# Swapped PSUM bank sets, and four more paired slabs whose combinations are made one by one

## The chip, the cores and the metric

One Trainium2 chip; the kernel runs on one of its cores. The metric is the device time of one execution in microseconds. TensorE (PE in the profile) multiplies, VectorE (DVE) and ScalarE (ACT) convert and add, GpSimd (POOL) and SyncE (SP) mostly issue DMAs.

## The reference

One layer of an encoder over 256 rows of width 2048, in float32: a group of mixers, a cross attention, and a gated MLP, each behind an RMS norm. The change touches the MLP and its last projection:

```python
D_FF = ((8 * D_MODEL // 3 + 255) // 256) * 256      # 5632

def swiglu(h, w_gate_up, w_down):
    gate, up = jnp.split(h @ w_gate_up, 2, axis=-1)
    return (jax.nn.silu(gate) * up) @ w_down
...
    x = x + swiglu(rms_norm(x, norm_g[l, 2]), w_gate_up[l], w_down[l])
return rms_norm(x, final_norm_g)
```

## The kernel before

**Slabs, halves and products.** All weights come in one stream of slabs of 128 x 2048 floats (1 MB), loaded by SP into three `raw` buffers. A slab is used as halves of up to 1024 columns. Each half is turned into two fp32r parts: ACT casts `raw` to `wh` (L135, or L159 in a paired slab), DVE subtracts to get the rest `wl` (L136, L160). A ring of three `wh`/`wl` buffers, and a fourth in an extra pool, lets these conversions run ahead of PE. The activations are split in the same way into a high and a low part. A product, `part` (L431), is three matmuls of 128 x 512: high by `wh` (L433), high by `wl` (L434), low by `wh` (L435).

**Plain and paired slabs.** In `paired_rows` (L452) a letter stands for a slab. N is plain: four row blocks by two halves of the 256 rows, eight products. S is paired: a block of 2 x 2 (two row blocks k, two column blocks) is multiplied by seven products instead of eight, in Strassen's manner. An S needs sums of weights, which `_sums` (L140) makes on DVE in place (L157, four additions of 128 x 512 in down's slabs, and conversions of 1024, 512, 1024 and 1024 columns), and sums of activations, the combination that `combine` (L438) makes of two activation tiles: two additions of 128 x 256, four of 128 x 128, then splits into a tile `z`. With the combination go four temporary tiles (`tmp`, eleven buffers). The second product of an S (`b0`, with `x4`) and the later ones use the combination; the first does not.

**Banks.** A group accumulates into eight PSUM banks: a0, a1, b0, b1 (two column blocks by two halves of the rows) from the pool psG (`gbank`, named pg in the profile), and the four products 1, 5, 6, 7 from psM (`bank`, named pm). When the last S of a group is through, `mixed` adds up 1, 5, 6 and 7; then `first` (`gated` in gate/up, `done` in down) adds a0 and a1; b0 and b1 are added after the group's last slab (`upped`, `done`).

**Gate/up.** After a first group by plain slabs, ten groups j = 1 to 10 follow the plan NNSNSNSN. Each ends in `up`: a product with the gate, a transpose, and a store to HBM. The tiles f[0] to f[43] of the hidden activations come back from there through `fetch` (POOL loads a `tmp`, ACT and DVE split it): 22 during gate/up, 22 during down.

**Down.** Two passes over the 44 tiles f, each for two of the four column blocks, by the two plans of `PASSES`. `rest` are the tiles that no S takes; the plain slabs run through them, first for column block 0, then for 1, and `ready(k)` sees to it that f[k + 2] is there. The last 12 rows of the last column block are held back for `down_end`: a part of x is added by matmuls with `identr` (L1230), then the held products run for row half 0 and row half 1, and the final norm follows each. `before(17)` of the second pass gives the extra buffer back.

**Order.** `Background` keeps generators (`fetch`, `combined`) with due times; `poll` steps one between products where less than OWED = 0.9 us of DVE work is owed by its own count, `drain` runs one to its end. What the code emits is then scheduled: instructions of an engine stand in the order in which a scheduler found them ready, earlier code first, not strictly in the order of the code. `keep_place` pins some.

Of the kernel before, what the change touches and what calls it, by code (L numbers as in the profile page):

```python
# [14 lines left out]
F32R = mybir.dt.float32r  # L15
# [8 lines left out]
P = 128  # L24
R = 256
D = 2048
KT = D // P
DFF = 5632
# [16 lines left out]
GROUP = "NNSNSNSN"  # L45

DOWN = GATE_UP + 80
PASSES = "NNNNNNSNNSNNSNNSNNSNNN", "NNSNSNSNSNSNSNNNNNNNNN"

PAIRED = {a + i for a, plan in [(GATE_UP + 8 * j, GROUP) for j in range(10)] + [(DOWN, PASSES[0]), (DOWN + 22, PASSES[1])]  # L50
          for i, x in enumerate(plan) if x == "S"}
# [153 lines left out]
class Background:  # L205
# [17 lines left out]
    def first(self, g):  # L223

        self.q.sort(key=lambda e: e[0] is not g)
# [29 lines left out]
class Block:  # L255
# [25 lines left out]
    def tt(self, out, a, b, op):  # L281
        self.bg.dve(math.prod(out.shape[1:]))
        self.nc.vector.tensor_tensor(out=out, in0=a, in1=b, op=op)  # L283
# [154 lines left out]
    def combine(self, z, a, b):  # L438

        tt, t, u, v, w = self.tt, *(self.tmp() for _ in range(4))  # L440
        for x, y in ((t, a), (u, b)):
            tt(x, y[:, 0:R].bitcast(F32), y[:, R:512].bitcast(F32), ALU.add)
        yield SOON
        tt(v[:, 0:P], t[:, P:R], u[:, P:R], ALU.subtract)
        tt(w[:, 0:P], t[:, 0:P], t[:, P:R], ALU.subtract)
        tt(v[:, P:R], v[:, 0:P], t[:, 0:P], ALU.subtract)
        tt(w[:, P:R], u[:, 0:P], v[:, P:R], ALU.add)
        yield SOON
        for i, x in enumerate((v, w)):
            self.split2(z[:, i * R:i * R + R], z[:, 512 + i * R:512 + i * R + R], x)  # L450

    def paired_rows(self, w, cols, slots, sums, plan, mixed, first, ready=None, late=0, before=None):  # L452

        st, s, nk = self.st, len(sums), len(slots)
        rest = [k for k in range(nk) if not any(k in ks for ks, _ in sums)]
        steps = [(c, k) for c in range(2) for k in rest]  # L460
        todo, q = iter(sums), {}
        count = {"a0": len(rest) + s, "a1": len(rest) + s, "b0": len(rest) + s, "b1": len(rest)}
        left, total = {}, 0

        def put(name, hi, lo, wh, wl):
            if name not in q:
                q[name] = self.gbank() if name in count else self.bank()
                left[name] = count.get(name, s)
            new = left[name] == count.get(name, s)
            left[name] -= 1  # L470
            self.part(q[name][:, :], hi, lo, wh, wl, new, left[name] == 0)

        form = lambda t, r: (t[:, r * P:(r + 1) * P], t[:, R + r * P:R + (r + 1) * P])
        n = done = 0
        for i, kind in enumerate(plan):
            if before:
                before(i)
            if kind == "S":
                ks, z = next(todo)
                a = [form(slots[ks[0]], 0), form(slots[ks[1]], 0), form(slots[ks[1]], 1)]  # L480
                x1, s2, s3, x4 = ((z[:, i * P:i * P + P], z[:, 512 + i * P:512 + i * P + P]) for i in range(4))
                t = (("5", x1), ("7", s3))
                pairs = iter((("1", a[0]), ("b0", x4), ("a0", a[1]), *(t if st.n // 16 in SUMMED else t[::-1]), ("a1", a[2]), ("6", s2)))
                for parts in st.take_sums(w, ks, cols):
                    for wh, wl in parts:
                        name, (hi, lo) = next(pairs)
                        put(name, hi, lo, wh, wl)
                        self.bg.poll()
                done += 1
                if done == s:  # L490
                    mixed(*(q[i] for i in "1567"))
            else:
                for c, k in steps[n:n + 4]:
                    if ready:
                        ready(k)
                    wh, wl = st.take(w, k, cols[c], 4)
                    for r in range(2):
                        put("ab"[c] + str(r), *form(slots[k], r), wh, wl)
                        self.bg.poll()
                n += 4  # L500
            if first and done == s and n >= len(rest):
                first(q["a0"], q["a1"])
                first = None
        assert n == len(steps) - late and done == s
        return [q["b0"], q["b1"]], rest[len(rest) - late:]
# [527 lines left out]
    def gate_up(self, gp, f, z):  # L1033

        nc = self.nc
        box, g, stored = {}, {}, []
# [6 lines left out]
        def up(j, ps, h=None):  # L1043
            h = h or [gp.tile([P, 512], F32, name="h", tag="h", bufs=2) for _ in range(2)]
            for r in range(2):
                self.stt(h[r], ps[r], box["col"][:, r:r + 1], g[r], ALU.mult, ALU.mult)
                self.store_turned(self.ff, 4 * j, r, g[r], h[r])
            stored.append(self.bg.now)
# [16 lines left out]
        def upped(j, ps):  # L1065

            for r in range(2):
                self.tt(h[r], h[r], ps[r], ALU.add)
            up(j, h, h)
# [34 lines left out]
        def combined():  # L1104
            for ks, z in sums:
# [3 lines left out]
        sums = [((2 * i, 2 * i + 1), z[i]) for i in range(GROUP.count("S"))]  # L1109
# [3 lines left out]
                            before=lambda n: n in (1, 3) and self.bg.drain(self.late if n == 1 else last))  # L1113
# [3 lines left out]
        early = self.bg.add(fetch(0, FT - 22, 3, 2.0, 15))  # L1117
        self.bg.drain(comb)
        for j in range(1, DFF // 512):
            upped(j, self.paired_rows("w_gate_up", [j * 512, DFF + j * 512], self.h3, sums, GROUP, mixed, gated)[0])  # L1120
        self.bg.drain(early)
        self.fetch = self.bg.add(fetch(FT - 22, FT, 6, SOON))

    def down(self, f, sp):

        nc, st = self.nc, self.st
        ss = self.rp.tile([P, 24], F32, name="rc", tag="rc")  # L1130
        self.gap(sp, 192)
        z = [sp.tile([P, 1024], F32R, name=f"y{i}") for i in range(PASSES[1].count("S"))]
        u = sp.tile([P, 512], F32, name="u")
        sums = [((2 * i, 2 * i + 1), x) for i, x in enumerate(z)]
        made, split = [], []

        def combined(n):
            for ks, x in sums[len(made):n]:
                yield from self.combine(x, *(f[k] for k in ks))
                made.append(x)  # L1140
                yield 2.0

        def squares(x, c, r):
            nc.scalar.activation(self.tmp().bitcast(BF16), x, AF.Square, accum_out=ss[:, 4 * r + c:4 * r + c + 1])

        def mixed(c, q1, q5, q6, q7):

            add = lambda a, b: self.tt(a, a, b, ALU.add)
            nc.scalar.copy(u, q1)
            add(self.half(c, 0), u)  # L1150
            add(u, q6)
            v = [(self.tmp(), slice(j, j + R)) for j in range(0, 512, R)]
            for t, j in v:
                self.tt(t, u[:, j], q7[:, j], ALU.add)
            self.tt(u, q5, u, ALU.subtract)
            add(self.half(c + 1, 0), u)
            for t, j in v:
                add(self.half(c, 1)[:, j], t)
                self.tt(t, q5[:, j], t, ALU.subtract)
                add(self.half(c + 1, 1)[:, j], t)  # L1160
            if c:
                for j in range(0, 512, R):
                    parts = [self.tmp().bitcast(F32R) for _ in range(2)]
                    self.split2(*parts, self.half(3, 1)[:, j:j + R])
                    split.append((j, parts))

        def done(c, *ps):

            for r, p in enumerate(ps):
                x = self.half(c, r)  # L1170
                self.tt(x, x, p, ALU.add)
                squares(x, c, r)

        def ready(k):

            while self.have < min(FT, k + 3):
                self.bg.step(next(e for e in self.bg.q if e[0] is self.fetch))

        for i, plan in enumerate(PASSES):
            n = plan.count("S")  # L1180
            g = self.bg.add(combined(n))
            late = (0, LATE)[i]
            plan = plan[:22 - late // 4]

            def before(j):
                if j == plan.index("S"):
                    self.bg.drain(g)
                if late and j == len(plan) - 2:
                    st.extra = None

            ps, rest = self.paired_rows("w_down", [2 * i * 512, (2 * i + 1) * 512], f, sums[:n], plan,
                                        lambda *q: mixed(2 * i, *q), lambda *q: done(2 * i, *q), ready, late, before)
            if i == 0:
                done(1, *ps)
        return ss, ps, rest, split
# [681 lines left out]
```

## Time and profile before

| | us |
|---|---|
| median of 3 runs | 1444.63 |
| runs | 1441.95 to 1446.84 |
| the profiled execution, time | 1443.87 |
| the profiled execution, span of instructions | 1442.1 |

The profile is of one execution; "idle before" and "[... <-X]" say how long the engine had been idle and what ended that. In the profile, down's fetched tiles appear under the names of the buffers that they lie in (act, f, z), combinations of down as y, the temporaries as tmp. The second pass begins at about 1317.4 us, the held end at 1417.2.

### The profile page before, as it was taken

What the parts mean: (1) busy time and instruction counts of PE and PEld (TensorE: products, weight loads), DVE (VectorE), ACT (ScalarE), POOL (GpSimd) and SP (SyncE); (2) the same over time, 40 slices, a digit from 0 to 9 for tenths busy, and PEclk for the clock granted to TensorE, in tenths of its full rate; (3) what the DMA queues carried; (4) which work ended last, traced back from release to release, by engine and by line L of the source; (5) the groups of instructions that cost most, each with busy time, mean ns of one, the idle gap of its engine ahead of it and who ended that gap; (6) DMA issues with size and microseconds to landing.
All of it is one profiled execution on the core that took longest, in us unless ns stands there. A gap on an engine that the chain in (4) does not pass through costs nothing.

```text
span 1442.1 us, 18599 instructions
## 1 busy us (share of the span) xinstructions
PE 1426.6 (99%) x6601; PEld 1183.1 (82%) x6601; DVE 1125.6 (78%) x1681; ACT 807.5 (56%) x1160; POOL 234.8 (16%) x306
## 2 busy tenths in 40 slices
PE   9999999999999999999999999999999999999997
PEld 8888888888888888888888888888888878788886
DVE  6667868777977666676676888889888889978884
ACT  7556655446655555555555555555555556555553
POOL 0000100012312233530421112112211103000000
PEclk9999999999999999999999999999999999999999
DMA  9886564456667788864976998989999877645563
GB/s 357 296 287 242 204 216 152 170 180 220 204 204 222 240 260 266 270 207 153 295 238 206 281 304 272 284 266 279 280 290 294 263 229 266 200 180 193 216 221 130
DMA packets 73039, 343.80 MB, mean 238 GB/s; under 512 B 10958, under 2 KB 12655, under 8 KB 45169
## 3 DMA queue, kind: packets, MB, share of 16 engines
q1 hardware_dynamic: 54848, 288.98, 57.4%
q0 software_dynamic: 17664, 52.97, 15.4%
q8 instruction: 52, 0.85, 0.2%
q10 hardware_dynamic: 432, 0.66, 0.1%
q14 instruction: 43, 0.34, 0.1%
HBM read 322.12 MB, written 20.45 MB: 238 GB/s over the span
## 4 chain that ended last, share of the span: by engine, by line
PE 93%; DVE 3%; DMA 2%; ACT 1%; issue 0%; ACTq 0%; DVEq 0%
PE pg L433 25%; PE pg L435 25%; PE pg L434 25%; PE pg L381 4%; DMA raw<-in_W 2%; PE pm L434 2%; PE pm L433 2%; PE pm L435 2%; PE pg L382 2%; DVE wl L136 1%; PE pm L1330 1%; PE pm L1008 1%; ACT wh L135 1%; PE pm L979 1%; DVE wl L160 0%
## 5 line engine op out<-in xcount | busy, mean ns | idle before, releaser
L136 DVE TENSOR_TENSOR wl<-raw,wh 128x1024 fp32r<-128x1024 f32 (+1 forms) x421 | 504.6, 1212 | 175.4 <-ACT wh L135 172.1
L135 ACT CAST wh<-raw 128x1024 fp32r<-128x1024 f32 (+1 forms) x421 | 433.2, 1043 | 303.1 <-PE pg L435 216.0
L433 PE MATMUL pg<-wh,act 128*128 128x512 f32 (+1 forms) x1454 | 567.9, 391 | 3.4 <-DVE g L283 3.3
L434 PE MATMUL pg<-wl,act 128*128 128x512 f32 (+1 forms) x1454 | 566.5, 390 | 2.1 <-DVE wl L160 1.1
L435 PE MATMUL pg<-wh,act 128*128 128x512 f32 (+1 forms) x1454 | 566.1, 390 | 0.5 <-DVE act L283 0.5
L433 PEld LDWEIGHTS pg<-wh,act 128*128 128x128 f32 x1454 | 273.3, 188 | 63.5 <-DVE g L283 5.9
L434 PEld LDWEIGHTS pg<-wl,act 128*128 128x128 f32 x1454 | 273.3, 188 | 59.1 <-DVE wl L136 2.3
L435 PEld LDWEIGHTS pg<-wh,act 128*128 128x128 f32 x1454 | 273.1, 188 | 58.2 <-DVE act L283 1.1
L159 ACT CAST wh<-raw 128x1024 fp32r<-128x1024 f32 (+1 forms) x134 | 122.4, 918 | 143.9 <-PE pg L435 82.9
L160 DVE TENSOR_TENSOR wl<-raw,wh 128x1024 fp32r<-128x1024 f32 (+1 forms) x134 | 139.0, 1058 | 63.4 <-ACT wh L159 63.1
L381 PE MATMUL pg<-act,wh 128*128 128x512 f32 x256 | 90.5, 395 | 0.0
L382 PE MATMUL pg<-act,wl 128*128 128x256 f32 x256 | 71.8, 280 | 0.0
L102 POOL DMA_DIRECT2D two<-in_W x30 | 26.6, 886 | 243.6 <-DMA two<-in_W 138.3
L159 ACT CAST wh<-two 128x1024 fp32r<-128x1024 f32 x30 | 31.5, 1051 | 52.6 <-PE pg L435 43.6
L381 PEld LDWEIGHTS pg<-act,wh 128*128 128x128 f32 x256 | 48.1, 188 | 10.5
L157 DVE TENSOR_TENSOR raw<-raw 128x512 f32<-128x512 f32 x74 | 51.1, 690 | 1.7
L550 POOL DMA_DIRECT2D tmp<-hidden x44 | 38.8, 889 | 58.3 <-issue 22.1
L382 PEld LDWEIGHTS pg<-act,wl 128*128 128x128 f32 x256 | 48.2, 188 | 0.2
L160 DVE TENSOR_TENSOR wl<-two,wh 128x1024 fp32r<-128x1024 f32 x30 | 36.7, 1223 | 7.2 <-ACT wh L159 7.1
L545 POOL DMA_DIRECT2D hidden<-g x22 | 17.2, 788 | 143.3 <-DVE g L543 143.3
L434 PE MATMUL pg<-wl,f 128*128 128x512 f32 x94 | 36.6, 389 | 0.0
L435 PE MATMUL pg<-wh,f 128*128 128x512 f32 x94 | 36.6, 389 | 0.0
(362 smaller groups left out, 1678.0 us busy)
## 6 DMA issues: line engine op xcount, KB each, us to landing
raw<-in_W SPq DMA_DIRECT2D x216, 1024.0 KB, 5.6
raw<-in_W SPq DMA_DIRECT2D x30, 768.0 KB, 6.7
two<-in_W SPq DMA_DIRECT2D x60, 256.0 KB, 5.0
two<-in_W POOLq DMA_DIRECT2D x30, 512.0 KB, 9.2
raw<-in_W SPq DMA_DIRECT2D x11, 512.0 KB, 7.2
hidden<-g POOLq DMA_DIRECT2D x22, 256.0 KB, 3.7
tmp<-hidden POOLq DMA_DIRECT2D x44, 128.0 KB, 5.5
features<-tmp POOLq DMA_DIRECT2D x32, 128.0 KB, 5.0
```

The source lines that it names most:

```text
L102: nc.gpsimd.dma_start(t, W[:, 512:1536], accum_op=ALU.add)
L135: nc.scalar.copy(wh[:, a:b], r[:, a:b])
L136: nc.vector.tensor_tensor(out=wl[:, a:b], in0=r[:, a:b], in1=wh[:, a:b].bitcast(F32), op=ALU.subtract)
L157: nc.vector.tensor_tensor(out=out, in0=a, in1=b, op=ALU.add)
L159: nc.scalar.copy(wh, src)
L160: nc.vector.tensor_tensor(out=wl, in0=src, in1=wh.bitcast(F32), op=ALU.subtract)
L381: self.nc.tensor.matmul(p[:, :], wh, slot[:, :], start=start, stop=False)
L382: self.nc.tensor.matmul(p[:, 0:R], wl, slot[:, 0:R], start=False, stop=stop)
L433: self.nc.tensor.matmul(p, hi, wh, start=start, stop=False)
L434: self.nc.tensor.matmul(p, hi, wl, start=False, stop=False)
L435: self.nc.tensor.matmul(p, lo, wh, start=False, stop=stop)
L550: self.nc.gpsimd.dma_start(t.rearrange("p (g t) -> p g t", t=32), src)
```

## The change

1. **Bank sets trade places.** `paired_rows` gets `swap`. With it, a0, a1, b0, b1 come from psM and 1, 6, 7, 5 from psG. It is on for gate/up's groups with even j and for down's second pass, so that neighbouring groups use the sets the other way round. The four banks of the products are taken together, in the order 1, 6, 7, 5, when the first of them is needed.
2. **More paired slabs in down.** Pass 0 has 6 S of 22 slabs instead of 5, the first at slot 4 instead of 6; pass 1 has 9 instead of 6, alternating with N, the last at slot 17 instead of 12 (of 19; the rest is held back). 15 S and 26 N instead of 11 and 30.
3. **Smaller combinations.** A tile for a combination in down has 768 columns instead of 1024, and there are eight; the ninth pair uses the first tile again. The fourth combination, `x4`, goes to the quarter of the pair's first activation tile that its seven products do not read.
4. **Combinations one by one.** Before a pass's first S, its combinations were drained together. Now, before each S, only as many steps are drained as that S needs.

```diff
-PASSES = "NNNNNNSNNSNNSNNSNNSNNN", "NNSNSNSNSNSNSNNNNNNNNN"
+PASSES = "NNNNSNNSNNSNNSNNSNNSNN", "NSNSNSNSNSNSNSNSNSNNNN"
...
-        for i, x in enumerate((v, w)):
-            self.split2(z[:, i * R:i * R + R], z[:, 512 + i * R:512 + i * R + R], x)
+        hi, lo, x4 = self.forms(z, a)
+        self.split2(hi[:, 0:R], lo[:, 0:R], v)
+        if hi.shape[1] == 512:
+            self.split2(hi[:, R:512], lo[:, R:512], w)
+        else:
+            self.split2(hi[:, R:], lo[:, R:], w[:, 0:P])
+            self.split2(*x4, w[:, P:R])
+
+    def forms(self, z, a):
+        n = z.shape[1] // 2
+        hi, lo = z[:, 0:n], z[:, n:2 * n]
+        return hi, lo, (hi[:, 384:512], lo[:, 384:512]) if n == 512 else (a[:, P:R], a[:, R + P:512])
...
         def put(name, hi, lo, wh, wl):
             if name not in q:
-                q[name] = self.gbank() if name in count else self.bank()
-                left[name] = count.get(name, s)
+                for x in [name] if name in count else "1675":
+                    q[x] = (self.bank if (name in count) == swap else self.gbank)()
+                    left[x] = count.get(x, s)
...
-                x1, s2, s3, x4 = ((z[:, i * P:i * P + P], z[:, 512 + i * P:512 + i * P + P]) for i in range(4))
+                hi, lo, x4 = self.forms(z, slots[ks[0]])
+                x1, s2, s3 = ((hi[:, i * P:i * P + P], lo[:, i * P:i * P + P]) for i in range(3))
...
-            upped(j, self.paired_rows("w_gate_up", ..., GROUP, mixed, gated)[0])
+            upped(j, self.paired_rows("w_gate_up", ..., GROUP, mixed, gated, swap=j % 2 == 0)[0])
...
-        z = [sp.tile([P, 1024], F32R, name=f"y{i}") for i in range(PASSES[1].count("S"))]
+        z = [sp.tile([P, 768], F32R, name=f"y{i}") for i in range(8)]
-        sums = [((2 * i, 2 * i + 1), x) for i, x in enumerate(z)]
+        sums = [((2 * i, 2 * i + 1), z[i % 8]) for i in range(PASSES[1].count("S"))]
...
             def before(j):
-                if j == plan.index("S"):
-                    self.bg.drain(g)
+                while plan[j] == "S" and len(made) <= plan[:j].count("S"):
+                    self.bg.step(next(e for e in self.bg.q if e[0] is g))
...
             ps, rest = self.paired_rows("w_down", ...,
-                                        ..., ready, late, before)
+                                        ..., ready, late, before, i == 1)
```

More of the change, by code (lines that the diff above doesn't have):

```diff
@@ L448, in combine, with paired_rows @@
         yield SOON
-        for i, x in enumerate((v, w)):
-            self.split2(z[:, i * R:i * R + R], z[:, 512 + i * R:512 + i * R + R], x)
-    def paired_rows(self, w, cols, slots, sums, plan, mixed, first, ready=None, late=0, before=None):
+        hi, lo, x4 = self.forms(z, a)
[9 more added lines that the diff above has]
+        return hi, lo, (hi[:, 384:512], lo[:, 384:512]) if n == 512 else (a[:, P:R], a[:, R + P:512])
+    def paired_rows(self, w, cols, slots, sums, plan, mixed, first, ready=None, late=0, before=None, swap=False):
         st, s, nk = self.st, len(sums), len(slots)
@@ L1119, in gate_up @@
         for j in range(1, DFF // 512):
-            upped(j, self.paired_rows("w_gate_up", [j * 512, DFF + j * 512], self.h3, sums, GROUP, mixed, gated)[0])
+            upped(j, self.paired_rows("w_gate_up", [j * 512, DFF + j * 512], self.h3, sums, GROUP, mixed, gated, swap=j % 2 == 0)[0])
         self.bg.drain(early)
@@ L1191, in down @@
             ps, rest = self.paired_rows("w_down", [2 * i * 512, (2 * i + 1) * 512], f, sums[:n], plan,
-                                        lambda *q: mixed(2 * i, *q), lambda *q: done(2 * i, *q), ready, late, before)
+                                        lambda *q: mixed(2 * i, *q), lambda *q: done(2 * i, *q), ready, late, before, i == 1)
             if i == 0:
```

## The prediction

> **What bounds the kernel now.** I read the page first: who is busy, at what clock, and what the chain of work that ended last is made of.
>
> ```profile
> span 1442.1 us, 18599 instructions
> PE 1426.6 (99%) x6601; PEld 1183.1 (82%) x6601; DVE 1125.6 (78%) x1681; ACT 807.5 (56%) x1160; POOL 234.8 (16%) x306
> PEclk9999999999999999999999999999999999999999
> PE 93%; DVE 3%; DMA 2%; ACT 1%; issue 0%; ACTq 0%; DVEq 0%
> ```
>
> TensorE sets the time, at full granted clock; the other 7% of the chain are the places where something else ended last. A busy PE is not yet a PE at its pace, so I take the pace from the timeline: two first matmuls (L433) of products that follow each other (three matmuls each).
>
> ```profile
> 1383.41 0.39 PE L433 MATMUL pm<-wh,y 128*128 128x512 f32 x1
> 1384.09 0.39 PE L433 MATMUL pg<-wh,act 128*128 128x512 f32 x1
> ```
>
> A product takes 0.68 us, whatever banks or operands it has. Next the busy time by stretches (columns: stretch, length, then each engine's busy time): gate/up group j = 1 alone; groups 2 to 10; down's first pass; the second pass to its last paired slab; the slabs after it; and the first half of the held end.
>
> ```profile
> core 0: us, PE busy (x) PEld busy (x) DVE busy (x) ACT busy (x) POOL busy (x), PEclk, DMA share, GB/s
> 777.60:819.10 41.50, 41.50 (x185) 34.36 (x184) 32.66 (x37) 21.64 (x24) 7.71 (x9) 1.00 0.84 257
> 819.10:1197.60 378.50, 375.09 (x1648) 308.66 (x1647) 324.41 (x384) 213.57 (x248) 60.11 (x70) 1.00 0.90 275
> 1197.60:1317.40 119.80, 117.20 (x514) 96.06 (x514) 103.41 (x158) 66.03 (x92) 12.98 (x15) 1.00 0.63 214
> 1317.40:1384.10 66.70, 66.70 (x296) 55.20 (x296) 59.25 (x74) 38.95 (x45) 0.00 (x0) 1.00 0.50 186
> 1384.10:1417.20 33.10, 33.10 (x149) 27.48 (x148) 24.14 (x37) 16.32 (x23) 0.00 (x0) 1.00 0.63 229
> ```
>
> A plain slab N is 8 products (5.44 us), a paired one S is 7 (4.76 us). A group NNSNSNSN is 61 products, 41.5 us: group 1 has exactly that. Nine more should take 373.4 us and take 378.5: 5.1 us are lost. Pass 0 (17 N, 5 S) is 171 products, 116.3 us, and takes 119.8: 3.5 us lost. The next stretch (7 N, 6 S, 98 products, 66.7 us) loses nothing. Who ended those waits, from the waits of PE:
>
> ```profile
> PE pg L433 <- DVE g L283: 3.3, 5, 1.0
> PE pg L434 <- DVE wl L160: 1.1, 1, 1.1
> PE pg L434 <- DVE wl L136: 1.0, 1, 1.0
> PE pg L435 <- DVE act L283: 0.5, 1, 0.5
> ```
>
> Five times PE waited for an addition g<-g,pg, that is for a bank of psG to come free (group boundaries); the wl and act waits lie at down's first paired slab.
>
> **Part 1, the bank sets.** The worst boundary (group 9 to 10), PE and DVE:
>
> ```profile
> 1154.65 0.68 DVE L283 TENSOR_TENSOR h<-pm,g 128x512 f32<-128x512 f32 x1
> 1156.41 1.23 DVE L136 TENSOR_TENSOR wl<-raw,wh 128x1024 fp32r<-128x1024 f32 x1 [1.09 <-ACT wh L135]
> 1157.56 0.68 DVE L283 TENSOR_TENSOR g<-g,pg 128x512 f32<-128x512 f32 x1
> 1158.29 0.50 PE L433 MATMUL pg<-wh,act 128*128 128x512 f32 x1 [0.99 <-DVE g L283]
> 1161.90 1.18 DVE L136 TENSOR_TENSOR wl<-raw,wh 128x1024 fp32r<-128x1024 f32 x1
> 1164.55 0.39 PE L434 MATMUL pg<-wl,act 128*128 128x512 f32 x1
> ```
>
> The next group's a1 needs the bank that the second `gated` addition still reads. That addition is queued on DVE behind a weight conversion which itself waits for ACT's cast. With the sets swapped, a0 and a1 of the next group get banks that `mixed` has read: its last read of pm is the row at 1154.65, over at 1155.33, while the blocking one ends at 1158.24; the additions before it free the other banks earlier. So the wait has nothing left to wait for at any of the nine boundaries. What is late next is the conversion at 1161.90: it ends at 1163.08, its user reads at 1164.55, so 1.47 us are in hand and the removed wait takes about 1.26 of them (0.99 idle, the rest in PE's restart). It just fits here, and this is the worst of the boundaries. The first paired slab of the swapped group needs all four psG banks two slabs (10.9 us) after the boundary; the last of them is read by `upped`, two additions behind 1157.56. No instruction is added. Gain 5.1 us, 4.0 if a little comes back in the conversion. Between the passes (bank sets swapped too) nothing was lost before, and the last psG read lies as far ahead of its next use: nothing.
>
> **Part 2, four more paired slabs.** 11 S become 15 and 30 N become 26: four products less, 4 x 0.68 = 2.7 us of PE. Loads are the same slabs, one 1 MB DMA each, so SP and its queue have nothing new; the 22 late fetches on POOL stay, asked for two rows earlier since the plain rows start at 12 and not 10. The price is on DVE. A steady N S period of pass 1:
>
> ```profile
> 1341.21 2.36 DVE L136 TENSOR_TENSOR wl<-raw,wh 128x1024 fp32r<-128x1024 f32 x2
> 1343.49 1.82 DVE L160 TENSOR_TENSOR wl<-raw,wh 128x1024 fp32r<-128x1024 f32 x2
> 1345.23 2.86 DVE L157 TENSOR_TENSOR raw<-raw 128x512 f32<-128x512 f32 x4
> 1348.01 1.22 DVE L160 TENSOR_TENSOR wl<-raw,wh 128x1024 fp32r<-128x1024 f32 x1
> 1350.33 1.23 DVE L160 TENSOR_TENSOR wl<-raw,wh 128x1024 fp32r<-128x1024 f32 x1 [1.10 <-ACT wh L159]
> 1351.47 1.22 DVE L136 TENSOR_TENSOR wl<-raw,wh 128x1024 fp32r<-128x1024 f32 x1
> ```
>
> An N costs 2.28 us (1341.21 to 1343.49). An S costs 1343.49 to 1349.15 and one more conversion of 1.14, that is 6.8. A pair: 9.1 of PE's 10.2 us, with about 1.1 idle. Passes of 16 N + 6 S and 10 N + 9 S add 4 x (6.8 - 2.28) = 18 us of DVE, and three more combinations. One combination (last three rows), from the one made in pass 1 and a split from pass 0, behind a conversion at the pass's start and its first reader:
>
> ```profile
> 1318.73 1.23 DVE L136 TENSOR_TENSOR wl<-raw,wh 128x1024 fp32r<-128x1024 f32 x1 [0.30 <-ACT wh L135]
> 1325.83 0.39 PE L434 MATMUL pg<-wl,f 128*128 128x512 f32 x1
> 1319.87 0.76 DVE L283 TENSOR_TENSOR tmp<-f 128x256 f32<-128x256 f32 x2
> 1320.68 1.02 DVE L283 TENSOR_TENSOR tmp<-tmp 128x128 f32<-128x128 f32 x4
> 1211.35 0.75 DVE L283 TENSOR_TENSOR y<-tmp,y 128x256 fp32r<-128x256 f32 x2
> ```
>
> That is 2.5 us, and 2.7 with the split in three pieces that the unused quarter asks for (ACT gets a third cast: 56% busy, hidden). Pass 1 now: nine pairs 9 x 9.1 = 81.9, three combinations 8.1, `done` of pass 0's last two banks 1.3: 91.3 us of DVE against 91.8 of PE. The pass begins with conversions ahead (done at 1319.96, read at 1325.83: 5.9 us, where 1 is enough), some 5 us to draw on, so it can hold, but with little to spare. The ninth combination overwrites the first tile after slot 1, and the quarters used by pairs 7 to 9 are last read as plain rows in pass 0: neither wait is near its due time. I put stalls here at 1.5 us (0 to 4).
>
> **Part 3, combinations one by one.** At pass 0's first S three combinations were drained in one go in front of a conversion:
>
> ```profile
> 1082.39 0.76 DVE L283 TENSOR_TENSOR tmp<-act 128x256 f32<-128x256 f32 x2
> 1233.50 0.42 DVE L283 TENSOR_TENSOR tmp<-f 128x256 f32<-128x256 f32 x1
> 1234.38 1.22 DVE L160 TENSOR_TENSOR wl<-raw,wh 128x1024 fp32r<-128x1024 f32 x1
> 1235.65 0.50 PE L434 MATMUL pg<-wl,act 128*128 128x512 f32 x1 [1.12 <-DVE wl L160]
> ```
>
> Sums of the fifth combination (the only tmp<-f of this pass) stand in front of the wl that PE waits for, though the fifth is used four S later. Now each S asks for its own one only, with two N between. The 3.5 us go, and what is late next is DVE itself in the first slots: pass 0 adds one S (+4.5) and one combination (+2.7) to 103.4 us busy, 110.6 of 115.7. I leave 1.0 us of stalls (0 to 2). A combination asked for at the last moment could stall its own S; but the order on DVE isn't the order of the code: the first two sums of pass 0 stand at 1082.39, 115 us ahead of the pass, as soon as inputs and tmp buffers are free. So late requests should be made in idle time before.
>
> **Part 4, a short end.** The last S moves from slot 12 to slot 17 of 19. `mixed` and `done` then have one N (5.44 us) before the matmuls with identr, which need the last split, where they had six.
>
> ```profile
> 1385.80 0.68 DVE L283 TENSOR_TENSOR u<-u,pm 128x512 f32<-128x512 f32 x1
> 1390.74 1.22 DVE L136 TENSOR_TENSOR wl<-raw,wh 128x1024 fp32r<-128x1024 f32 x1
> 1394.07 0.42 DVE L283 TENSOR_TENSOR tmp<-res,tmp 128x256 fp32r<-128x256 f32 x1
> ```
>
> From the first sum after the S to the last split: 8.7 us, two conversions among them. With one conversion fewer in the queue before it and one fewer within: 7.6, begun 1.7 - 1.1 = 0.6 after the S ends (1384.09): 8.2, so PE waits 2.7 us there, and the held products behind it. The lower bound: if PE's order puts the first held products ahead, DVE still has 6.4 + 6 conversions x 1.14 + 0.5 = 13.7 us to do before the last held half, which PE reaches 5.44 + 0.5 (identr) + 5 x 1.36 = 12.7 us after the S: 1.0. I take 2.6, nearest to the order seen.
>
> **Sum.** -5.1 - 2.7 - 3.5 + 1.5 + 1.0 + 2.6 = -6.2 us. The profiled execution took 1443.87 us (span 1442.1 and 1.8 around it), 0.8 under the median 1444.63; so 1437.7 to 1438.4: **1438**. Its own range, all bounds: -5.1 - 2.7 - 3.5 + 1.0 = -10.3 (1433.6) to -4.0 - 2.7 - 3.5 + 4 + 2 + 2.7 = -1.5 (1442.4). What this kernel's runs can tell from no change is about 0.3%, 4.3 us.
>
> **Rivals.** (a) The late requests stay late: each combination of pass 1 is made behind the third conversion of its own S. That ends at 1349.23, 0.5 us into an S; 2.7 more, and the S's second product, due at 0.68, waits 2.0 to 2.5. Three of them 6 to 7, and about 1 each for three in pass 0, in place of my 1.5 + 1.0: 1438 + 4 to 8 = 1442 to 1445. For it: the planner steps a combination unasked only while it counts under 0.9 us of owed DVE work, and 9.1 of 10.2 us leave it little. Against: the row at 1082.39. (b) The boundary wait returns as a wait for weights: DMA is 0.90 busy in that stretch and the conversion has 0.2 us in hand at the worst boundary. If each boundary gives its wait back, 1438 + 5 = 1443: no change to be measured. (c) DVE becomes the bound, and it is slower. Suppose it can use none of the idle time that it shows, since that is spent in front of conversions whose cast is late (as at 1350.33) and whatever is put there moves the next conversion. Pass 0 was idle for 119.8 - 103.4 = 16.4 us: 110.6 + 16.4 = 127.0 against 115.7, 11.3 over. Pass 1: a pair costs 10.2, combinations and `done` 9.4 on top. Of 20.7 us the 5 ahead and my 2.5 come off: 1438 + 13 = 1451, slower by 0.45%. With half of the idle time usable it is 3.1 + 4.3 - 5 - 2.5, nothing; it makes the kernel slower from about nine tenths unusable. For it: 91.3 of 91.8. Against: the sums of a combination take 0.2 to 0.4 us each and fit in gaps of 1.1.
>
> The Trainium skill's page VectorE: DVE Perf Modes, section The DRAIN you can't avoid, has a rule that speaks for (c): the next operation does not start until the pipe of the one before is empty. By it rows would add up with their full durations. Here they do not where operations follow freely: two conversions of 1.22 take 2.36, so the trace shows 0.08 us less each; by the rule pass 1 would need about 4 us more of DVE (five such pairs in each of nine periods), an estimate that would make 1442. Since the row contradicts it, it gets no chance of its own.
>
> **Chances.** Forecast 0.70, (a) 0.13, (b) 0.07, (c) 0.10. Faster by over 0.3% (below 1440.3): most of the forecast's own range, 0.64; within: its upper end, (a) and (b), 0.26; slower (over 1449): (c), 0.10. The range 1433.5 to 1445 holds the forecast's own and (a) and (b).
>
> **What would show it.** Right: no PE wait on g L283 in 819 to 1193, groups of 41.5 us throughout; PE 12 matmuls fewer; no cluster of tmp sums before a wl at the first S; one wait of 1 to 3 us at L1230 or just behind it; DVE over 95% busy in pass 1. Wrong: PE waits at pm or pg for wl at most S of pass 1 (c), or for a combination's split at the second product of slots 13, 15 and 17 (a); waits on wl 8 us into the groups (b).

## The result, and the profile after

| | before | after |
|---|---|---|
| median, same chip | 1445.74 (6 runs, 1441.95 to 1450.35) | 1436.72 (6 runs, 1435.07 to 1439.0) |
| the profiled execution | 1443.87 | 1435.07 |
| its span | 1442.1 | 1433.3 |

The changed kernel takes 0.9942 of the time before, with a 95% interval of 0.9922 to 0.9963. The page of the profiled execution after, the same four lines as before:

```profile
span 1433.3 us, 18652 instructions
PE 1423.0 (99%) x6589; PEld 1180.7 (82%) x6589; DVE 1146.2 (80%) x1738; ACT 815.2 (57%) x1183; POOL 234.8 (16%) x306
PEclk9999999999999999999999999999999999999999
PE 97%; DVE 1%; ACT 0%; DMA 0%; issue 0%; SPq 0%; ACTq 0%
```

PE has the 12 matmuls less that four products make (6601 to 6589), VectorE has 20.6 us more work, and in the chain that ended last PE's share rises from 93 to 97%. Busy time by stretches, in the columns of before: group j = 1, groups 2 to 10, pass 0, pass 1, the held end, the rest.

```profile
777.70:819.20 41.50, 41.50 (x185) 34.38 (x184) 32.67 (x37) 22.22 (x25) 7.71 (x9) 1.00 0.86 259
819.20:1193.10 373.90, 373.83 (x1649) 308.90 (x1648) 324.26 (x384) 212.12 (x247) 60.13 (x70) 1.00 0.90 279
1193.10:1309.70 116.60, 116.57 (x511) 95.32 (x510) 107.65 (x177) 68.33 (x102) 12.98 (x15) 1.00 0.63 213
1309.70:1407.00 97.30, 97.30 (x431) 80.54 (x431) 93.39 (x133) 56.69 (x69) 0.00 (x0) 1.00 0.57 208
1407.00:1424.60 17.60, 17.45 (x77) 13.76 (x75) 15.01 (x34) 10.39 (x21) 0.00 (x0) 1.00 0.16 61
```

Nine groups take 373.9 us where before they took 378.5; pass 1 runs on PE without a gap although VectorE is busy 93.39 of 97.30 us. All waits of PE that the view lists for the whole execution:

```profile
PE pm L601 <- DVE eps L602: 1.1, 1, 1.1
PE pg L434 <- DVE wl L136: 0.2, 1, 0.2
```

None is for a bank, and both lie ahead of the ten groups. The view leaves out very short waits; what the table below says is lost in after is made of such ones. The table has the stages of every profiled execution. Each is worked out from the starts of the L434 matmuls that begin it and the next stage. "Lost" is its length less products x 0.6801 us, the pace that the gapless stages show (three starts, 0.2267 us apart); for the ten groups it is the length less 414.80, which is what three gapless executions took. The matmuls with identr cost 0.48 us wherever they stand.

| kernel | ten groups | lost | pass 0 | lost | pass 1 | held end | both, lost beside identr | tail | time |
|---|---|---|---|---|---|---|---|---|---|
| before | 420.03 | 5.2 | 119.81 | 3.51 | 99.77 | 16.33 | 0.0 | 8.55 | 1443.87 |
| after | 415.39 | 0.6 | 116.65 | 1.04 | 97.24 | 17.55 | 0.7 | 8.74 | 1435.07 |
| swap_only | 419.79 | 5.0 | 119.77 | 3.48 | 99.77 | 16.33 | 0.0 | 8.55 | 1443.60 |
| no_swap | 422.03 | 7.2 | 116.63 | 1.02 | 97.24 | 17.57 | 0.8 | 8.75 | 1442.68 |
| after_again | 416.02 | 1.2 | 116.44 | 0.82 | 97.24 | 17.55 | 0.7 | 8.74 | 1435.96 |
| no_swap_again | 419.81 | 5.0 | 116.63 | 1.02 | 97.24 | 17.57 | 0.8 | 8.72 | 1439.44 |
| old_plan | 417.40 | 2.6 | 116.28 | 0.0 | 99.77 | 16.33 | 0.0 | 8.55 | 1437.95 |
| drain_first | 421.07 | 6.3 | 123.21 | 7.59 | 97.24 | 17.57 | 0.8 | 8.72 | 1447.35 |
| rawx | 414.80 | 0.0 | 116.30 | 0.68 | 97.24 | 17.57 | 0.8 | 8.64 | 1436.99 |
| rawx_no_swap | 414.80 | 0.0 | 116.32 | 0.70 | 97.24 | 17.57 | 0.8 | 8.64 | 1434.15 |
| asked_only | 415.55 | 0.7 | 118.22 | 2.60 | 97.24 | 17.57 | 0.8 | 8.63 | 1437.27 |
| asked_pinned | 418.22 | 3.4 | 122.51 | 6.89 | 103.91 | 17.67 | 7.5 | 8.63 | 1451.47 |
| held_pinned | 416.31 | 1.5 | 116.36 | 0.74 | 101.41 | 16.34 | 3.7 | 8.72 | 1438.81 |
| rawx_best | 414.80 | 0.0 | 116.28 | 0.0 | 98.41 | 16.33 | 0.0 | 8.52 | 1434.19 |

Two things stand out. Down's stages repeat to 0.35 us in all kernels that share their code (pass 0: 116.30 to 116.65), so one execution settles them. The ten groups do not. In the seven kernels whose lines for these groups are those of after (after, after_again, old_plan, drain_first, asked_only, asked_pinned, held_pinned) they lost 0.6 to 6.3 us, 2.3 in the mean; without the swap (before, no_swap, no_swap_again) 5.0 to 7.2, 5.8 in the mean. There only repeated timings count. (In rawx's profiled execution the groups began 3 us later than in rawx_no_swap, which has the same buffers; for rawx the median is the number to use.)

### The profile page after: what moved, and what is told of

It is laid out like the page before. It is cut to its first block, busy times and chain, and to the rows that moved or that the text cites. A ratio compares the mean times of both kernels' runs of the same rounds, so it can differ in the third digit from the quotient of the medians.

```text
span 1433.3 us, 18652 instructions
## 1 busy us (share of the span) xinstructions
PE 1423.0 (99%) x6589; PEld 1180.7 (82%) x6589; DVE 1146.2 (80%) x1738; ACT 815.2 (57%) x1183; POOL 234.8 (16%) x306
## 4 chain that ended last, share of the span: by engine, by line
PE 97%; DVE 1%; ACT 0%; DMA 0%; issue 0%; SPq 0%; ACTq 0%
PE pg L433 22%; PE pg L434 22%; PE pg L435 22%; PE pm L434 7%; PE pm L435 7%; PE pm L433 7%; PE pg L381 4%; PE pg L382 2%; PE pm L1344 1%; PE pm L1022 1%; PE pm L993 1%; DMA raw<-in_W 0%; PE pm L1753 0%; DVE res L283 0%; PE pm L994 0%
## 5 line engine op out<-in xcount | busy, mean ns | idle before, releaser
L136 DVE TENSOR_TENSOR wl<-raw,wh 128x1024 fp32r<-128x1024 f32 (+1 forms) x413 | 494.8, 1212 | 166.1 <-ACT wh L135 163.2
L433 PE MATMUL pg<-wh,act 128*128 128x512 f32 (+1 forms) x1191 | 465.6, 391 | 0.0
L434 PE MATMUL pg<-wl,act 128*128 128x512 f32 (+1 forms) x1191 | 463.9, 389 | 0.4 <-DVE wl L136 0.2
L435 PE MATMUL pg<-wh,act 128*128 128x512 f32 (+1 forms) x1191 | 463.9, 389 | 0.0
L433 PEld LDWEIGHTS pg<-wh,act 128*128 128x128 f32 x1191 | 223.8, 188 | 47.8 <-issue 1.5
L434 PEld LDWEIGHTS pg<-wl,act 128*128 128x128 f32 x1191 | 223.8, 188 | 47.2 <-DVE wl L136 1.3
L435 PEld LDWEIGHTS pg<-wh,act 128*128 128x128 f32 x1191 | 223.7, 188 | 47.2 <-DVE act L283 0.4
L160 DVE TENSOR_TENSOR wl<-raw,wh 128x1024 fp32r<-128x1024 f32 (+1 forms) x150 | 156.1, 1061 | 57.0 <-ACT wh L159 56.8
L434 PE MATMUL pm<-wl,act 128*128 128x512 f32 x309 | 120.5, 390 | 0.1
L433 PE MATMUL pm<-wh,act 128*128 128x512 f32 x309 | 120.2, 389 | 0.0
L435 PE MATMUL pm<-wh,act 128*128 128x512 f32 x309 | 120.2, 389 | 0.0
L434 PEld LDWEIGHTS pm<-wl,act 128*128 128x128 f32 x309 | 58.0, 188 | 13.0 <-DVE wl L136 0.6
L433 PEld LDWEIGHTS pm<-wh,act 128*128 128x128 f32 x309 | 58.0, 188 | 12.0
L435 PEld LDWEIGHTS pm<-wh,act 128*128 128x128 f32 x309 | 58.0, 188 | 12.0
L157 DVE TENSOR_TENSOR raw<-raw 128x512 f32<-128x512 f32 x90 | 62.0, 689 | 1.3
```

The source lines that it names most:

```text
L136: nc.vector.tensor_tensor(out=wl[:, a:b], in0=r[:, a:b], in1=wh[:, a:b].bitcast(F32), op=ALU.subtract)
L157: nc.vector.tensor_tensor(out=out, in0=a, in1=b, op=ALU.add)
L160: nc.vector.tensor_tensor(out=wl, in0=src, in1=wh.bitcast(F32), op=ALU.subtract)
L433: self.nc.tensor.matmul(p, hi, wh, start=start, stop=False)
L434: self.nc.tensor.matmul(p, hi, wl, start=False, stop=False)
L435: self.nc.tensor.matmul(p, lo, wh, start=False, stop=stop)
```

## The experiments

**The swap alone, and all but the swap.** `swap_only` is the kernel before with the exchange of bank sets in gate/up; `no_swap` is the changed kernel without it:

```diff
-            upped(j, self.paired_rows(..., gated, swap=j % 2 == 0)[0])
+            upped(j, self.paired_rows(..., gated)[0])
```

> The kernel before with the swapped bank sets in gate/up alone (down as before). Theory: the wait at the boundaries was for a psG bank and nothing else is late there, so the ten groups from 777.6 us on take 415.4 us as after the change (they took 420.0) and the time falls by 4.6 us, about 0.3%; down's first pass keeps its 119.8 us with the same waits for wl. Rival: the boundary wait comes back as a wait for weights, which are late with DMA 90% busy; then the groups take 418 to 420 us and the time stays.

> The changed kernel without the swap in gate/up (down keeps its own). Theory: the five or six waits for g<-g,pg come back, the groups take 420 us again, down is as after the change (pass 0 116.7 us, no wait in pass 1), and the time rises by 4.6 us, to about 1441. Rival: the new order in down has moved the waits, and the groups stay near 415.

Measured on one chip, where the kernel before had 1444.58 (14 runs): swap_only 1440.76 (10 runs), ratio 0.9978 (0.9968 to 0.9987); no_swap 1438.52 (5 runs), ratio 0.9959 (0.9944 to 0.9974). swap_only gained 3.8 us, near the 4.6 expected, but its profiled execution, the second slowest of the ten, kept 5.0 us of loss in the groups: there the rival's sign came. no_swap came out lower than the 1441 expected. The waits of PE in gate/up, first of no_swap, then of swap_only:

```profile
PE pg L433 <- DVE g L283: 4.9, 6, 2.6
```

```profile
PE pm L434 <- DVE wl L136: 1.6, 2, 0.8
PE pg L434 <- DVE wl L136: 0.7, 1, 0.7
PE pm L434 <- DVE wl L160: 0.3, 1, 0.3
```

So the swap removes the wait for a bank, every time. In its place stands a wait for weights about 8 us into a group: rival (b). How it comes about, in the timeline of swap_only:

```profile
1113.05 1.05 ACT L135 CAST wh<-raw 128x1024 fp32r<-128x1024 f32 x1 [5.38 <-DMA raw<-in_W]
1114.13 1.23 DVE L136 TENSOR_TENSOR wl<-raw,wh 128x1024 fp32r<-128x1024 f32 x1 [1.65 <-ACT wh L135]
1114.63 1.03 ACT L135 CAST wh<-raw 128x1024 fp32r<-128x1024 f32 x1
1118.39 1.30 DVE L544 STREAM_TRANSPOSE g<-h 128x512 f32<-128x512 f32 x2
1119.61 1.18 DVE L136 TENSOR_TENSOR wl<-raw,wh 128x1024 fp32r<-128x1024 f32 x1
1120.85 0.50 PE L434 MATMUL pg<-wl,act 128*128 128x512 f32 x1 [0.71 <-DVE wl L136]
```

ACT waited 5.38 us for a load of weights. That load was asked for at 1104.68, when the conversion of an older slab had freed its `raw` buffer, and landed 8.3 us later, at 1112.95. The cast for the second half was done at 1115.66, but by then VectorE had begun the additions and transposes that end the group before, and the conversion came only at 1119.61, after them. PE waited for that. The bank wait of before had the same beginning. At its worst boundary the blocking addition stood behind a conversion whose cast was late, and of that cast the profile says:

```profile
1155.33 1.05 ACT L135 CAST wh<-raw 128x1024 fp32r<-128x1024 f32 x1 [4.44 <-DVE h L283]
```

It names an addition that ends at 1155.33, but the load that the cast reads, asked for at 1147.25, landed at 1155.23, as far ahead of its cast as in swap_only (0.10 us). With the fourth buffer of the next experiment neither wait is left. The swap does not make the load come earlier; it gives PE some more microseconds before the delay reaches it.

**The same pair again, and a load that comes earlier.** What the swap is worth was timed with both versions on one chip, and the supposed origin was taken away by a fourth `raw` buffer in gate/up (its room taken from the tiles `ar`, three in place of four), with the swap (`rawx`) and without (`rawx_no_swap`). Every fourth slab uses the new buffer, in all groups but the last:

```diff
-        self.raw = self.rawp.tile([P, 2048], F32, name="raw", tag="raw")
+        self.raw = (self.rawx if self.rawx and n // 16 % 4 == 3 else self.rawp).tile([P, 2048], ...)
...
-        arrival = lambda: gp.tile([P, R], F32, name="ar", tag="ar", bufs=4)
+        arrival = lambda: gp.tile([P, R], F32, name="ar", tag="ar", bufs=3)
```

> The changed kernel once more, timed on one chip beside the next three. The stages of down should repeat to 0.1 us (pass 0 116.7, pass 1 97.2, held end 17.6), the groups of gate/up should not: they took 415.4, 417.4, 419.8 and 421.1 us in four profiles with the swap. Theory: what varies is how late a slab's load lands; here 415 to 421, all waits for wl, none for a bank. Rival (the swap removes the loss, the others were another chip): 415.4 again.

> The changed kernel without the swap in gate/up, once more beside it on the same chip. Theory (the swap gives PE a little over a microsecond of slack at a boundary where a load lands late, and no more): groups 419 to 423 us, waits for g<-g,pg, and a median 2 to 3 us over the changed kernel's. Rival, my prediction's step: 5 us over it. Second rival, the swap does nothing: within 1 us.

> The changed kernel with a fourth buffer for raw slabs during gate/up (each fourth slab uses it; one of four small arrival buffers is given up for the room). Theory: PE's waits in the groups come from loads that are issued when a buffer comes free and land late; issued a slab (5 us) earlier they are in time, every group takes 41.5 us, the ten 414.8, and the time falls by what the groups lose now, 1 to 6 us, with less spread. Rival: DVE's load at the boundary delays the conversions whatever the landing; then the groups still take 417 to 421 us.

> The fourth raw buffer without the swap in gate/up. Theory of the loads: the conversion in front of the second gate addition is no longer late, so the bank is free in time too: no wait for g<-g,pg, groups 414.8 us, the time as with the fourth buffer and the swap. Rival, the bank itself is the cause: the bank waits stay and the groups take 419 to 420 us.

| one chip, before at 1443.34 (17 runs) | median | runs | ratio to before |
|---|---|---|---|
| no_swap_again | 1439.22 | 12, 1436.99 to 1441.88 | 0.9970 (0.9960 to 0.9980) |
| after_again | 1436.56 | 6, 1435.80 to 1437.56 | 0.9952 (0.9935 to 0.9969) |
| rawx | 1434.76 | 4, 1434.33 to 1436.99 | 0.9942 (0.9922 to 0.9961) |
| rawx_no_swap | 1434.27 | 4, 1434.06 to 1435.65 | 0.9937 (0.9918 to 0.9956) |

The swap is worth 1439.22 - 1436.56 = 2.7 us in the new kernel (1.7 to 3.6, an interval worked out from the runs) and 3.8 in the old one, by swap_only (1.9 to 4.6 by its ratio's interval). The buffer brings another 1.8 with the swap, which so few runs do not tell from nothing, and a clear 5.0 without it. The waits of ACT for plain slabs' loads in gate/up, of before, after, swap_only and no_swap, in this order (us in total, times, longest):

```profile
ACT wh L135 <- DMA raw<-in_W: 21.0, 7, 4.2
```

```profile
ACT wh L135 <- DMA raw<-in_W: 15.7, 5, 4.3
```

```profile
ACT wh L135 <- DMA raw<-in_W: 31.0, 9, 5.4
```

```profile
ACT wh L135 <- DMA raw<-in_W: 25.2, 8, 6.2
```

And what rawx_no_swap has left, with its nine groups by the windows:

```profile
ACT wh L135 <- DMA raw<-in_W: 1.9, 1, 1.9
819.30:1192.60 373.30, 373.30 (x1648) 309.22 (x1647) 323.86 (x384) 214.61 (x246) 60.01 (x70) 1.00 0.90 276
```

In rawx this row is missing altogether. With the loads asked for a slab earlier PE loses nothing in the groups, with the bank sets in either order. The order of the banks was thus not the origin of the loss in gate/up, only the place where a late load came to light first.

**The old plan, and the old drain.** `old_plan` is the changed kernel with the plans of before (171 and 146 products); `drain_first` is the changed kernel with all six combinations of pass 0 made before its first S:

```diff
             def before(j):
+                while i == 0 and j == plan.index("S") and len(made) < n:
+                    self.bg.step(next(e for e in self.bg.q if e[0] is g))
```

> The changed kernel with the old plans of the passes (5 and 6 paired slabs of 22), all else as after the change. Theory of the products: four products more, 2.7 us; the first pass has 171 products, 116.3 us, and nearly no wait since the combinations are no longer drained together, so it takes 116.5 to 117.3; the held end has its six plain slabs again and no wait, 0.7 us less. In sum 1.5 to 2.5 us more than the changed kernel. Rival: the drain was not what stalled PE, DVE's whole load was; then pass 0 loses 2 us or more again.

> The changed kernel with all six combinations of pass 0 drained together before its first paired slab, at slot 4. Theory: the burst of some 13 us of DVE work stands in front of conversions, and PE waits 3 to 6 us there (it lost 3.5 with the old plan); pass 0 takes 119 to 122 us instead of 116.7. Rival: the order on DVE is the scheduler's, not the code's, and it spreads the combinations anyway; pass 0 stays under 117.5.

old_plan loses nothing in pass 0 (116.28 us for 171 products), where before lost 3.51: with the combinations made one by one the 3.5 are gone. (old_plan has the smaller tiles and the swaps too; drain_first, below, changes the drain alone.) Its down part is 240.93 us (99.77, 116.28, 16.33 and 8.55), that of after 240.18: the four products less, 2.72 us, bring only 0.75, since after loses 1.04 in pass 0, 0.74 in the held end and 0.19 in the tail; 1.5 to 2.5 had been expected. drain_first, one run, loses 7.59 in pass 0, more than the 3 to 6 expected. Its waits of PE there:

```profile
PE pg L434 <- DVE wl L136: 1.9, 1, 1.9
PE pg L434 <- DVE wl L160: 1.2, 1, 1.2
PE pg L435 <- DVE act L283: 1.1, 1, 1.1
PE pm L433 <- ACT wh L159: 0.7, 1, 0.7
```

The wait for wl and act at the first S is the one that before showed, and with six combinations and a start two slots earlier it costs twice as much.

**Are late requests made late?** In after, combination 7 stands among the conversions of the first two S of pass 1 and is complete over 40 us ahead of slot 13, which asks for it. VectorE's timeline of after, where its dependent sums lie singly between the four additions L157:

```profile
1322.34 0.68 DVE L157 TENSOR_TENSOR raw<-raw 128x512 f32<-128x512 f32 x1
1322.94 0.28 DVE L283 TENSOR_TENSOR tmp<-tmp 128x128 f32<-128x128 f32 x1
1323.15 0.68 DVE L157 TENSOR_TENSOR raw<-raw 128x512 f32<-128x512 f32 x1
1323.75 0.28 DVE L283 TENSOR_TENSOR tmp<-tmp 128x128 f32<-128x128 f32 x1
1323.95 0.68 DVE L157 TENSOR_TENSOR raw<-raw 128x512 f32<-128x512 f32 x1
1324.55 0.41 DVE L283 TENSOR_TENSOR y<-tmp,y 128x256 fp32r<-128x256 f32 x1
```

`asked_only` takes the planner's own steps away, so that a combination enters the code only where its S asks; `asked_pinned` also keeps it in the instruction order at that place:

```diff
+                e = next((e for e in self.bg.q if e[0] is g), None)
                 while plan[j] == "S" and len(made) <= plan[:j].count("S"):
-                    self.bg.step(next(e for e in self.bg.q if e[0] is g))
+                    mark = self.mark()        # asked_pinned only
+                    self.bg.step(e)
+                    self.keep_place(mark)     # asked_pinned only
+                if e:
+                    e[1] = 1e9
```

> The changed kernel with the planner's polling of the combinations taken out: a combination is put into the program only where its own paired slab asks for it, all its sums and splits in one go. In the changed kernel the pass 1 combinations stand in DVE's queue at 1313 to 1363, far ahead of slots 13, 15 and 17, and pass 1 takes 97.24 us without a wait. Theory: that comes from the order in which the instructions are placed, which takes sums as soon as their inputs are there, and not from the planner's steps; then pass 1 stays at 97.2 (0 to 0.3 over its 143 products) and pass 0 at 116.3 to 117.0. Rival, the prediction's (a): asked late means made late; each of the three combinations of pass 1 costs 2.0 to 2.5 us (pass 1 103 to 105), with PE waits for splits of tmp and y, and pass 0 takes 3 to 6 us more for its six.

> As asked_only, and each combination's instructions are kept at the place where they are asked for, that is at the head of their own paired slab, with nothing after them placed ahead of them or they ahead of what is before. This measures the price that the prediction's rival (a) put on a late combination. By (a): 2.0 to 2.5 us for each of three in pass 1 (97.2 becomes 103 to 105), about 1 each in pass 0, with PE waits for splits. If pass 1 stays under 99, late making would not have cost what (a) said, and the early place in the queue is not what saved the change.

One run each. asked_only has the same pass 1 to the hundredth, 97.24 us, with its tmp sums at the same places between the additions (the first 3.4 us into the pass, as in after); pass 0 loses 2.6 in place of 1.0. asked_pinned loses 6.66 us in pass 1, 2.2 for each of three combinations, and 6.89 in pass 0, 1.15 for each of six; it took 1451.47. Rival (a) had 2.0 to 2.5 and about 1. Where it waits in pass 1:

```profile
PE pm L434 <- DVE wl L160: 2.5, 2, 1.3
PE pm L433 <- ACT wh L135: 0.7, 1, 0.7
PE pm L434 <- DVE wl L136: 0.5, 1, 0.5
PE pg L433 <- ACT y L299: 0.3, 1, 0.3
```

(a) expected the wait at the splits. In two of the three S most of it is at the S's fourth conversion, which stands behind the pinned sums on VectorE, and in the third at a cast; its price was right. So a late combination does cost what (a) said, and what kept it from being late is the order of the instructions, which lets later code's sums go ahead as soon as their inputs and buffers are free.

**The held end.** PE in after puts held products ahead of and between the matmuls with identr; `held_pinned` keeps them behind, as the code has them:

```diff
+            mark = self.mark()
             ...                      # the held products
+            self.keep_place(mark)
```

> The changed kernel with the held products kept behind the matmuls with identr on PE, as the code has them. In the changed kernel PE's order puts three of the held products' matmul groups ahead of and between the identr ones, and the held end takes 17.55 us where 16.8 would be products alone. The prediction priced the wait for the last split at 2.7 us if identr stands first and at 1.0 otherwise. Theory: the order is what made it small; pinned, the held end takes 18.5 to 19.6 us, with a PE wait of 1.7 to 2.8 at L1244. Rival: DVE's own work up to the last held conversion sets this end, and the place of the wait does not matter: 17.5 to 17.9.

PE around the identr matmuls, first after, then held_pinned:

```profile
1408.35 0.28 PE L1244 MATMUL pm<-tmp,identr 128*128 128x256 f32 x1
1408.46 0.39 PE L433 MATMUL pm<-wh,act 128*128 128x512 f32 x1
1408.92 0.50 PE L434 MATMUL pm<-wl,act 128*128 128x512 f32 x1
...
1410.55 0.77 PE L1244 MATMUL pm<-tmp,identr 128*128 128x256 f32 x2
```

```profile
1408.87 0.39 PE L1244 MATMUL pm<-tmp,identr 128*128 128x256 f32 x1 [0.93 <-ACT tmp L299]
1410.38 0.38 PE L1244 MATMUL pm<-tmp,identr 128*128 128x256 f32 x1 [1.13 <-DVE tmp L283]
1411.26 0.84 PE L1244 MATMUL pm<-tmp,identr 128*128 128x256 f32 x2 [0.49 <-ACT tmp L299]
```

Pass 1 and the held end together are 114.79 us in after and 117.75 in held_pinned, 2.96 more, though both have the same work: waiting for the splits costs PE 3.7 us (2.55 of them are the idle times in the rows), and PE's order hides 3.0 of it behind held products. The rival (VectorE sets this end whatever the order) is out. The idle time is within the 1.7 to 2.8 expected; the cost is above them.

**A version from the parts that lose nothing.** `rawx_best` is rawx with pass 0's plan of before and eight S in pass 1, 13 S in all:

```diff
-PASSES = "NNNNSNNSNNSNNSNNSNNSNN", "NSNSNSNSNSNSNSNSNSNNNN"
+PASSES = "NNNNNNSNNSNNSNNSNNSNNN", "NSNSNSNSNSNSNSNSNNNNNN"
```

> rawx (the changed kernel with a fourth raw buffer in gate/up) with the plans that lose nothing: pass 0 as before with 5 paired slabs, pass 1 with 8 (the last S in slot 15 instead of 17), so 13 where the change has 15. Theory: two products more (1.36 us), but pass 0 gives up its 0.7 to 1.0 us of stall and the held end its 0.7: down's part 0.0 to 0.6 us shorter than the changed kernel's, time within 0.5 us of rawx, 1433.8 to 1434.8. Rival: pass 0 and the held end stall as before the change of plans, for causes other than the paired slabs, and it is 1.0 to 1.4 us slower than rawx, about 1436.

It took 1434.12 (4 runs, 1433.76 to 1434.19; before on that chip 1442.2, 7 runs), ratio 0.9938 (0.9922 to 0.9955): within what rawx and rawx_no_swap showed on another chip. Its down part is 239.54 us against 239.75 in rawx, with two products more. From pass 0 to the held end PE loses nothing but identr:

```profile
1192.80:1309.10 116.30, 116.30 (x514) 96.28 (x513) 103.38 (x163) 66.52 (x97) 12.96 (x15) 1.00 0.64 220
1309.10:1407.50 98.40, 98.40 (x437) 81.54 (x436) 94.15 (x140) 59.42 (x78) 0.00 (x0) 1.00 0.54 199
1407.50:1423.80 16.30, 16.30 (x74) 13.34 (x72) 8.91 (x18) 6.17 (x11) 0.00 (x0) 1.00 0.37 128
```

The last two paired slabs that the change adds are thus worth no more than they cost. Of what was run, the three versions with the buffer are the fastest, and the runs don't tell them apart.

## Why the prediction was right, and where not

The forecast was 1438.0 with a sum of -6.2; the medians moved by -9.0 on the first chip and by -6.8 on the one with most runs. Term by term, with what the runs give:

| term | forecast | measured | from |
|---|---|---|---|
| part 1, bank waits | -5.1 (-4.0 to -5.1) | -2.7, -3.8 | medians of after_again and no_swap_again; of before and swap_only |
| part 2, four products | -2.7 | -2.7 | 12 matmuls less at 0.2267 |
| part 3, the drain | -3.5 | -3.5 | old_plan, pass 0 |
| pass 1's stalls | +1.5 (0 to 4) | 0.0 | after, pass 1 |
| pass 0's stalls | +1.0 (0 to 2) | +0.7 to +1.0 | after, after_again, rawx |
| held end | +2.6 (1.0 to 2.7) | +0.7, and 0.2 in the tail | after |
| sum | -6.2 | -8.4 to -7.0 | |

**Part 1 is the step that failed**, by its size: 2.7 is outside its own bounds, 3.8 just under them, and neither of their intervals reaches 5.1. It said that the wait "has nothing left to wait for", which is so, and that the next thing, the conversion about 8 us into the group, "just fits", and that the worst boundary seen is the worst there is. But the lateness differs from execution to execution: no_swap's longest bank wait was 2.6 us where before's was 1.0, and the swap leaves a part of that as a wait for wl. That is rival (b), given 0.07 and the whole 5 us; between a quarter and a half of it came true. In the profiled execution of after hardly anything is seen of it (0.6 us lost in ten groups), so the sign announced for being right, groups of 41.5 us throughout, came by luck of that execution, the fastest of its six: the seven executions with this code lost 2.3 us in the mean, and the medians of after_again and rawx differ by 1.8. The reason that the prediction gave for the wait, an addition queued behind a conversion that itself waits for ACT's cast, was right as far as it went; it stopped short of the load that the cast waits for, and of the buffer that the load waits for.

**Pass 1** was forecast as tight, 91.3 us of work in 91.8. It was: VectorE is busy 96% of it. But it loses nothing, and combination 9, which the code asks for at slot 17, was made by slot 10. Rival (a) was refuted for the reason that the prediction gave against it, and asked_pinned shows that its price was right. Rival (c), that idle time in front of conversions cannot be used, is out: the sums lie in it one by one. The Trainium skill's page VectorE: DVE Perf Modes, section The DRAIN you can't avoid, lets no operation start before the pipe of the one before is empty, and adds that one which is not held starts earlier. By its rule alone this pass would be longer than its matmuls: the durations of its VectorE rows add up to 101.9 us, and it took 97.24. Here too rows of 0.68 and 0.28 start 0.60 and 0.21 apart (1322.34, 1322.94, 1323.15), and the measurement decides.

**The held end** took the bound that the prediction named and did not choose: PE's order does put held products ahead, and 0.7 us remain, under the 1.0 given; the announced wait of 1 to 3 us at identr does not appear. With the order that it chose as likelier, held_pinned shows 3.7 where it had priced 2.6 to 2.7. **Pass 0** and the drain came out as priced.

By the prediction's own terms the four paired slabs were to cost more in stalls (1.5 + 1.0 + 2.6) than the 2.7 us that they save. Measured, they are a small gain: down is 0.75 us shorter in after than in old_plan.

So part 1's gain was put 1.3 to 2.4 us too high, and the stalls 1.5 too high in pass 1 and 1.7 at the end. That these errors nearly cancel in the total was luck.

## What to carry to other kernels

When an engine waits for a buffer or a bank, follow the releaser back until the chain reaches something that nothing holds up any more: here bank, addition, conversion, cast, load, and the buffer that the load goes to. Where two releasers end within a tenth of a microsecond, look at both. A fix at the first link (other banks) is worth only the slack up to the next link, 2.7 to 3.8 of 5 us; one more buffer at the last link made all the waits vanish. And for a wait that has its origin in memory traffic, one profiled execution is a single sample: ask how its size varies before taking its slack at the worst place as given.

Code that asks late is not work done late where instructions are ordered by readiness; look in the timeline for where a later step's first instructions already stand.

## What the runs showed of the hardware

Loads of 1 MB take very different times. From issue to landing, as far as the trace tells the landing, those of plain slabs in gate/up took 4.8 to 9.2 us in before (median 7.1), 4.8 to 10.8 in swap_only (7.7), 4.7 to 9.3 in after_again (7.1), worked out load by load. Part of that is the place: in the eleven profiles with three `raw` buffers, a load asked for within 6 us of the one before the last took 7.5 us or more. But the same load of the same code differs too, by up to 3.6 us between the seven executions: the one asked for at 853.03 in after took 6.4 us, in asked_pinned 9.5; the one at 1175.26 took 7.9, in the six others 4.7 to 5.0. Over the whole of swap_only the median is 5.5, as its page's row of DMA issues says (KB each, median us to landing):

```profile
raw<-in_W SPq DMA_DIRECT2D x216, 1024.0 KB, 5.5
```

The DMA engines are 90% busy in the groups. With the same code what PE lost there went from 0.6 to 6.3 us from one execution to the next, while pass 0, pass 1 and the held end, with the DMA engines 65% busy or less, repeat to 0.35. The Trainium skill's page DMA: Bandwidth & Descriptors, section Latency and other measured facts, gives the latency of an access to HBM as 0.2 us on average and 2 us at high load. The direction agrees (7.7 us in the busy groups, 5.5 over all); no run here shows the latency of a single access, so the sizes can't be compared.
